# A shift of 224 bytes for the split weights that TensorE holds

## The chip, the cores and the metric

The kernel runs on one core of one Trainium2 chip. The core has a matrix engine (TensorE, PE in the profile; its weight loads are shown apart as PEld), a vector engine (VectorE, DVE), an activation engine (ScalarE, ACT), GpSimd (POOL) and a queue engine (SyncE, SP) that issues most DMAs. The on-chip memory SBUF has 128 partitions; a "byte offset" below always means an offset within each partition. The metric is the device time of one execution in microseconds (us); smaller is better.

## What is computed

Two transformer layers run over 256 tokens of width 2048, batch 1. Cut to what matters:

```python
# layer 1
hn = rms_norm(h, norm_mix);  h = h + nsa_mixer(hn, ...)            # compressed/selected/window attention
hn = rms_norm(h, norm_ffn);  h = h + square(relu(hn @ ffn_w1)) @ ffn_w2     # 2048 -> 8192 -> 2048
gate = sigmoid(rms_norm(h, norm_ple) @ ple_w_gate);  h = h + (p @ ple_w_proj) * gate
x = rms_norm(h, norm_final)
# layer 2
x = x + rms_norm(swa_sink_attention(rms_norm(x, g0), ...), g1)     # window 128, 32 heads
x = x + rms_norm(conv_ffn(rms_norm(x, g2), w_up, conv, w_down), g3)  # 2048 -> 2*5632 -> 2048
```

All is float32, and the products have to be nearly of float32 precision. Nearly all the work is products of the 256 token columns with about 400 MB of weights, each weight used once.

## The kernel before

The weights lie in DRAM as one stream of 128 x 128 tiles in the order of their use (`_stream`). `Weights.load` brings 16 tiles (1 MB) at a time into `w_raw`. `Weights.split` takes units of 8 tiles and writes each as two float32r numbers into one of four `w_split` buffers: the rounded value `hi` (ScalarE, L243) and the rest `lo` (VectorE, L244). A buffer holds 8 tiles of `hi` (4096 bytes) and behind them 8 tiles of `lo` (4096 bytes). The activations are split likewise: a `slot`, `h` or `o` tile holds 256 columns of `hi` and 256 of `lo`. A product is then hi·hi + hi·lo + lo·hi.

TensorE multiplies a stationary operand (128 columns, brought into the array by a LDWEIGHTS) with a moving one (up to 512 columns that stream past it). Three helpers use the weights:

- `mm` (L296 to L303): the weight tile is stationary and the activations move. Each tile costs one **pair**: `hi` held against 512 columns (L302), then `lo` held against 256 (L303). The result comes out transposed, as the next layer's input needs it. 3152 pairs.
- `mm_beside` (L305 to L313): the same with four output banks side by side, at the start of both feed-forward parts. 128 pairs.
- `mm_rows` (L315 to L325; `mm_rows_last` L327 to L337): the activations are stationary, and 4 weight tiles (512 columns) move, three matmuls for each half of the tokens. In `compress` (L809) the weights move too.

While a matmul streams, the LDWEIGHTS of the next one runs beside it. Tiles' places are set by pools in order of allocation. `pad` tiles (L457, L504, L560, L606, L610, L1098) fill up to multiples of 256 bytes (`ALIGN`): in the built program `w_split`, `slot`, `h`, `o`, `q`, `kh` and `vh` all begin at a multiple of 256 bytes, so that the stationary and the moving operand of every `mm`, `mm_beside` and `mm_rows` matmul stand at the same offset modulo 256, namely 0. Constants such as the identity stand at 224.

`hz` (L858, L1120) is the hidden activation before its split into `h`; it lies in the pool `base`, two buffers, through `tmp`.

The order on each engine is the order of the code, with a few places moved by `issue_after`.

Of the kernel before, what the change touches and what calls it, by code (L numbers as in the profile page):

```python
# [13 lines left out]
P = 128  # L14
S = 256
# [29 lines left out]


ALIGN = 256


V_MIX, V_FFN, V_PLE, V_FIN = 0, 16, 32, 48  # L50
# [44 lines left out]
    return [(i, NFF2 + i) for i in range(q * QUART, (q + 1) * QUART)]  # L95


def _stream(a):

    w = a["nsa_w_in"][0]  # L100
    kv = {n: w[:, 2048 + 512 * i : 2560 + 512 * i] for i, n in enumerate(("kc", "vc", "ks", "vs", "kw", "vw"))}
    out = [_g_major(kv["vs"]), _g_major(kv["vw"])]
    gates = np.zeros((KD, P, P), np.float32)
    gates[:, :, :48] = w[:, 5120:5168].reshape(KD, P, 48)
    out.append(gates)
    tiles = [_m_major(kv[n]).reshape(G, KD, P, P) for n in ("kc", "vc", "ks", "kw")]
    q = _m_major(w[:, :2048]).reshape(4 * G, KD, P, P)
    w1k, w1v = (a[f"nsa_cmp_w1_{n}"][0].reshape(4, CMP_L // 4, P, P) for n in "kv")
    out += list(tiles[0])
    for c in range(4):  # L110
        out += [tiles[1][c], w1k[c]]
    for c, t in enumerate((tiles[2][0], tiles[3][0], q[0], q[1])):
        out += [t, w1v[c]]
    out += list(q[2:4])
    for g in range(1, G):
        out += [tiles[2][g], tiles[3][g], *q[4 * g : 4 * g + 4]]
    out.append(_g_major(a["nsa_w_out"][0]))
    for h in range(2):
        w = a["ffn_w1"][0][:, h * 4096 : (h + 1) * 4096]
        if h == 0:  # L120
            out.append(_g_major(w[:, :COLS]))
            w = w[:, COLS:]
        out.append(_m_major(w))
        out.append(_g_major(a["ffn_w2"][0][h * 4096 : (h + 1) * 4096]))
    gate = _g_major(a["ple_w_gate"][0]).reshape(NG, -1, P, P)
    proj = _g_major(a["ple_w_proj"][0]).reshape(NG, -1, P, P)
    out.append(np.concatenate([gate, proj], axis=1).reshape(-1, P, P))
    w = a["swa_w_in_2"][0]
    order = _swa_order()
    out.append(_g_major(w[:, 2560:3072]))  # L130
    out.append(_m_major(w[:, 2048:2560]))
    out.append(_m_major(w[:, :2048][:, order]))
    out.append(_g_major(a["swa_w_out_2"][0][order]))
    up = a["ffn_w_up_2"][0].reshape(KD, P, 2 * NFF2, P)
    down = a["ffn_w_down_2"][0]

    def ups(pairs):
        return up[:, :, [m for pair in pairs for m in pair]]

    first = _conv_tiles(0)  # L140
    out.append(ups(first[:2]).transpose(0, 2, 1, 3).reshape(-1, P, P))
    out.append(ups(first[2:]).transpose(2, 0, 1, 3).reshape(-1, P, P))
    for q in range(4):
        nxt = _conv_tiles(q + 1) if q < 3 else []
        if nxt:
            out.append(ups(nxt[:1]).transpose(2, 0, 1, 3).reshape(-1, P, P))
        out.append(_g_major(down[q * QUART * P : (q + 1) * QUART * P]))
        if nxt:
            out.append(ups(nxt[1:]).transpose(2, 0, 1, 3).reshape(-1, P, P))
    n = sum(len(b) for b in out)  # L150
    pad = -n % 16
    flat = np.concatenate(out + [np.zeros((pad, P, P), np.float32)])
    return np.ascontiguousarray(flat.reshape(-1, 16, P, P).transpose(0, 2, 1, 3)).reshape(-1, P, 16 * P), n


def _cols(v):
# [50 lines left out]
class Weights:  # L207


    def __init__(self, nc, pool, src, blocks):  # L210
        self.nc, self.pool, self.src = nc, pool, src
        self.n, self.units = src.shape[0], -(-blocks // UNIT)
        self.at = self.n_dma = self.n_split = 0
        self.raw, self.both = {}, {}
# [18 lines left out]
    def split(self, upto):  # L233
        nc = self.nc
        while self.n_split < min(upto, self.units):
            u = self.n_split
            self.load(u // 2 + 1)
            raw = self.raw[u // 2][:, (u % 2) * UNIT * P : (u % 2 + 1) * UNIT * P]
            both = self.pool.tile([P, 2, UNIT * P], F32R, tag="w_split", name=f"w_split{u}", bufs=W_SPLIT)
            hi, lo = both[:, 0], both[:, 1]  # L240
            half = UNIT * P // 2
            for c in (slice(0, half), slice(half, 2 * half)) if u == 0 else (slice(0, 2 * half),):
                nc.scalar.activation(hi[:, c], raw[:, c], AF.Copy)  # L243
                nc.vector.tensor_tensor(lo[:, c], raw[:, c], hi[:, c].bitcast(F32), op=ALU.subtract)  # L244
            self.both[u] = both
            self.n_split += 1
            if u % 2:
                self.raw.pop(u // 2)
                self.load(u // 2 + 1 + W_RAW)
# [14 lines left out]


class Program:
    def __init__(self, tc, ins, out, blocks):
        self.tc, self.nc, self.ins, self.out, self.blocks = tc, tc.nc, ins, out, blocks
        self.uid = 0


# [180 lines left out]
    def build(self):  # L452
        tc, nc, ins = self.tc, self.nc, self.ins
        self.base = tc.alloc_tile_pool(name="base", bufs=1)
        self.psum = tc.alloc_tile_pool(name="psum", bufs=1, space=bass.MemoryType.PSUM)
        self.dram = tc.alloc_tile_pool(name="dram", bufs=1, space=bass.MemoryType.DRAM)
        self.pad(self.base, 64)  # L457
        self.w = Weights(nc, self.base, ins["w"], self.blocks)

        self.vecs = self.tile(self.base, [P, NV], F32, "vecs")  # L460
        cst = self.tile(self.base, [P, NC_], F32, "cst")
        self.ident = cst[:, C_ID : C_ID + P]
        self.ones = cst[:, C_ONE : C_ONE + P]
        self.fold = cst[:, C_FOLD : C_FOLD + 64]
        self.mask = cst[:, C_MASK : C_MASK + S]
        self.cmask = cst[:, C_CMASK : C_CMASK + 32].rearrange("p (b n) -> p b n", b=2)
        self.cvalid = cst[:, C_CVALID : C_CVALID + 32].rearrange("p (b n) -> p b n", b=2)

        self.eps = self.tile(self.base, [P, 1], F32, "eps")
        nc.vector.memset(self.eps, EPS)  # L470
        nc.scalar.dma_start(self.vecs[:, :KD], ins["vec"][:, :KD])
        self.x_pool = x_pool = tc.alloc_tile_pool(name="x0", bufs=1, side="right")
        x0 = [self.tile(x_pool, [P, 2, S], F32, f"x{i}") for i in range(KD // 2)]

        def load_x(i):
            nc.sync.dma_start(x0[i], ins["x"][:, 2 * i : 2 * i + 2])

        self.w.load(W_RAW, load_x)
        for i in range(2 * W_RAW, KD // 2):
            load_x(i)  # L480
        nc.scalar.dma_start(cst, ins["cst"])
        nc.scalar.dma_start(self.vecs[:, KD:], ins["vec"][:, KD:])


        idle = self.tile(x_pool, [P, COLS], F32R, "idle")
        nc.vector.memset(idle.bitcast(F32), 0.0)
        ps = self.ps_mm()
        for i in range(WARM):
            nc.tensor.matmul(ps, lhsT=idle[:, :P], rhs=idle, start=True, stop=True)


        xs = []
        acc = self.tile(x_pool, [P, S], F32, "acc")
        self.ps_vs = [self.ps_att(), self.ps_att()]
        for k in range(KD):
            src = x0[k // 2][:, k % 2]
            if k % 2 == 0:
                self.w.split(k // 2 + 1)
            x = self.slot(k, F32R)
            self.split512(x, src, self.vec(V_MIX + k))  # L500
            self.add_square(acc, src, k == 0)
            xs.append(x)
            self.mm_rows(self.ps_vs, [x], k == 0, k == KD - 1)
        self.pad(self.base, 96)  # L504
        self.nsa(xs, acc)
        self.ffn()
        self.ple()
        self.swa()
        self.conv_ffn()
        for pool in (self.pool_z, self.pool_y, self.dram, self.psum, self.base):  # L510
            pool.release()
        assert self.w.at == self.blocks
# [325 lines left out]
    def ffn(self):  # L838
# [8 lines left out]
        for part in range(2):  # L847
            hs = []
            beside = self.mm_beside(xs) if part == 0 else []
            for m in range(half):  # L850
                if m < len(beside):
                    ps = beside[m]
                else:
                    ps = self.ps_mm()
                    self.mm(ps, xs)
                z = self.total(ps)
                h = self.tmp("hz", 2)
                nc.vector.scalar_tensor_tensor(h, z, 0.0, z, op0=ALU.max, op1=ALU.mult)  # L858
                hr = self.tile(pool, [P, 512], F32R, f"h{m}")
                self.split512(hr, h)  # L860
                hs.append(hr)
# [229 lines left out]
    def conv_ffn(self):  # L1091
# [23 lines left out]
        def hidden(i, ps_g, ps_v):  # L1115
            cg, cv = conv(ps_g, i), conv(ps_v, NFF2 + i)
            sg = self.tile(pool, [P, S], F32, "sg", 2)
            nc.scalar.activation(sg, cg, AF.Silu)
            h = self.tmp("hz", 2)
            nc.vector.tensor_tensor(h, sg, cv, op=ALU.mult)  # L1120
            hs[i] = self.tile(pool, [P, 512], F32R, "h", QUART + 3)
            self.split512(hs[i], h)
# [97 lines left out]
```

## Time and profile before

| what | value |
|---|---|
| time, median of 3 runs | 2269.18 us (2268.64 to 2269.22) |
| time of the profiled execution | 2269.81 us |
| its span, first to last instruction | 2268.0 us |
| mean granted TensorE clock | 0.997 of full speed |
| matmuls of `mm` (L302, L303) | 3152 and 3152 |
| matmuls of `mm_rows` (L323 to L325) | 4032 |
| busy, PE / DVE / ACT / POOL | 99% / 64% / 52% / 11% |

PE is the engine that is busy all the time; DVE and ACT follow with the split of the weights. A matmul's duration in the profile holds its way through the array, so consecutive ones overlap: the pace of a stream is the distance from start to start, not the duration.

### The profile page before, as it was taken

The page shows a single profiled execution, that of the slowest core. Times are in us where ns is not written, and L with a number is a line of the kernel's source. Part 1 is how long each engine was busy: PE and PEld are TensorE (multiplying, and loading weights), DVE is VectorE, ACT ScalarE, POOL GpSimd, SP SyncE. Part 2 cuts the span into 40 slices and gives each one's busy share as a digit, 9 for nine tenths or more (in the row PEclk, how much of TensorE's full clock was granted, in tenths as well). Part 3 has the DMA queues.
Part 4 walks back from the last instruction along what each step waited for, and adds up shares of the span by engine and source line. Part 5 has one row for each costly group of instructions (what it writes and reads, how often), then busy time and mean ns, then how long its engine had stood idle before and what let it go on. Part 6 is the DMA issues. An engine that isn't in the chain of part 4 may idle for free. (4 is left out here: it accounts for less than half of the span.)

```text
span 2268.0 us, 29986 instructions
## 1 busy us (share of the span) xinstructions
PE 2236.1 (99%) x11645; PEld 1892.5 (83%) x11645; DVE 1447.1 (64%) x2181; ACT 1181.1 (52%) x1894; POOL 243.2 (11%) x309
## 2 busy tenths in 40 slices
PE   8999999999999999999999999999999999999998
PEld 6888887888888888888888888778888888888886
DVE  7676665566544566644566777567756766765775
ACT  4566554444433444444465566456545544554554
POOL 5432210000000000000001123002100100110110
PEclk9999999999999999999999999999999999999999
DMA  6553335555555555555555544445555555555553
GB/s 254 196 199 127 123 128 213 185 201 186 196 192 191 197 186 187 186 186 188 212 191 185 204 142 165 167 147 189 187 195 189 188 186 186 186 189 200 186 186 130
DMA packets 65950, 415.64 MB, mean 183 GB/s; under 512 B 7408, under 2 KB 12528, under 8 KB 17424
## 3 DMA queue, kind: packets, MB, share of 16 engines
q1 hardware_dynamic: 65376, 413.01, 50.5%
q8 instruction: 91, 1.49, 0.2%
q10 hardware_dynamic: 432, 0.73, 0.1%
q14 instruction: 51, 0.42, 0.0%
HBM read 410.03 MB, written 3.67 MB: 182 GB/s over the span
## 5 line engine op out<-in xcount | busy, mean ns | idle before, releaser
L244 DVE TENSOR_TENSOR w_split<-w_raw,w_split 128x1024 fp32r<-128x1024 f32 (+1 forms) x759 | 946.4, 1248 | 641.9 <-ACT w_split L243 636.4
L243 ACT ACTIVATE w_split<-w_raw 128x1024 fp32r<-128x1024 f32 (+1 forms) x759 | 801.6, 1057 | 699.4 <-PE att L325 447.9
L302 PE MATMUL mm<-slot,w_split 128*128 128x512 f32 x3152 | 1117.3, 399 | 1.5 <-DVE z L346 1.5
L303 PE MATMUL mm<-slot,w_split 128*128 128x256 f32 x3152 | 885.2, 281 | 0.0
L302 PEld LDWEIGHTS mm<-slot,w_split 128*128 128x128 f32 x3152 | 592.0, 188 | 149.8 <-issue 3.4
L303 PEld LDWEIGHTS mm<-slot,w_split 128*128 128x128 f32 x3152 | 595.3, 189 | 0.3
L324 PE MATMUL att<-w_split,h 128*128 128x512 f32 x848 | 330.2, 389 | 0.0
L325 PE MATMUL att<-w_split,h 128*128 128x512 f32 x848 | 330.2, 389 | 0.0
L323 PE MATMUL att<-w_split,h 128*128 128x512 f32 x848 | 330.1, 389 | 0.0
L344 ACT ACTIVATE t<-mm 128x256 f32<-128x256 f32 x201 | 76.4, 381 | 228.5 <-PE mm L303 227.0
L325 PEld LDWEIGHTS att<-w_split,h 128*128 128x128 f32 x848 | 159.2, 188 | 33.1
L324 PEld LDWEIGHTS att<-w_split,h 128*128 128x128 f32 x848 | 159.2, 188 | 32.9
L323 PEld LDWEIGHTS att<-w_split,h 128*128 128x128 f32 x848 | 159.2, 188 | 32.8
L1107 POOL TENSOR_TENSOR u<-z,rb 128x256 f32<-128x256 f32 x88 | 71.0, 808 | 694.3 <-DVE z L346 585.3
L346 DVE TENSOR_TENSOR z<-mm,t 128x256 f32<-128x256 f32 x201 | 84.8, 423 | 79.8 <-ACT t L344 79.8
L324 PE MATMUL att<-w_split,slot 128*128 128x512 f32 x320 | 125.9, 393 | 4.0 <-DVE w_split L244 3.9
L323 PE MATMUL att<-w_split,slot 128*128 128x512 f32 x320 | 125.2, 393 | 1.8 <-ACT w_split L243 1.7
L325 PE MATMUL att<-w_split,slot 128*128 128x512 f32 x320 | 125.7, 393 | 0.0
L919 POOL MEMSET vh<- 128x512 f32 x1 | 0.5, 524 | 910.1 <-DVE sum L391 910.1
L324 PEld LDWEIGHTS att<-w_split,slot 128*128 128x128 f32 x320 | 60.4, 189 | 19.2 <-DVE w_split L244 6.8
L323 PEld LDWEIGHTS att<-w_split,slot 128*128 128x128 f32 x320 | 60.3, 189 | 15.1 <-ACT w_split L243 3.0
L325 PEld LDWEIGHTS att<-w_split,slot 128*128 128x128 f32 x320 | 60.4, 189 | 12.2
(261 smaller groups left out, 1901.0 us busy)
## 6 DMA issues: line engine op xcount, KB each, us to landing
w_raw<-in_w SPq DMA_DIRECT2D x376, 1024.0 KB, 4.8
bias<-bandd SPq DMA_DIRECT2D x32, 128.0 KB, 2.7
w_raw<-in_w SPq DMA_DIRECT2D x5, 512.0 KB, 7.6
x<-in_x SPq DMA_DIRECT2D x8, 256.0 KB, 6.9
slot<-in_xn SPq DMA_DIRECT2D x8, 256.0 KB, 7.9
gain<-in_rows SPq DMA_DIRECT2D x2, 1024.0 KB, 6.1
out<-slot SPq DMA_DIRECT2D x8, 256.0 KB, 2.0
bandd<-rows SPq DMA_DIRECT2D x2, 768.0 KB, 6.4
```

The lines of the kernel that those rows point to most:

```text
L243: nc.scalar.activation(hi[:, c], raw[:, c], AF.Copy)
L244: nc.vector.tensor_tensor(lo[:, c], raw[:, c], hi[:, c].bitcast(F32), op=ALU.subtract)
L302: nc.tensor.matmul(ps, lhsT=hi, rhs=x, start=i == 0, stop=False)
L303: nc.tensor.matmul(ps[:, S:], lhsT=lo, rhs=x[:, :S], start=False, stop=i == n - 1)
L323: nc.tensor.matmul(ps[b], lhsT=xh, rhs=hi, start=first and i == 0, stop=False)
L324: nc.tensor.matmul(ps[b], lhsT=xh, rhs=lo, start=False, stop=False)
L325: nc.tensor.matmul(ps[b], lhsT=xl, rhs=hi, start=False, stop=last and i == n - 1)
L344: nc.scalar.activation(t, ps[:, S : 2 * S], AF.Copy)
L346: nc.vector.tensor_tensor(z, ps[:, :S], t, op=ALU.add)
L919: nc.gpsimd.memset(t[:, :, :, 64:128].bitcast(F32), 0.0)
L1107: nc.gpsimd.tensor_tensor(u[:, 2:], self.total(ps), rb, op=ALU.mult)
```

## The change

Each unit of 8 tiles gets a mark, `held`: 1 if its weights will be stationary (used by `mm` or `mm_beside`), 0 if they will move (`mm_rows`, `compress`). `_stream` returns the marks beside the data; the data and their order are the same. A `w_split` buffer grows by 256 bytes, from 8192 to 8448, and a unit with mark 1 is written, and then read, 56 floats (224 bytes) further on in it. Units with mark 0 stay at the buffer's start. To make room, `hz` moves from the pool `base` into the pools of the two feed-forward stages, again with two buffers.

In the built program the order of the instructions on each of the five engines is the same as before, row for row. The operands of matmuls keep their offsets modulo 256, save the held weights, which go from 0 to 224, both `hi` and `lo`. `hz` goes from 96 to 0. One wait is placed otherwise: the first `hz` of the first feed-forward waits for POOL as well as for DVE, and the first `h` behind it waits no longer for POOL.

```diff
+SHIFT = 56
 def _stream(a):
-    out = [_g_major(kv["vs"]), _g_major(kv["vw"])]
+    out.add(0, _g_major(kv["vs"]), _g_major(kv["vw"]))
-    out.append(gates)
+    out.add(1, gates)
...
-        out.append(_m_major(w))
-        out.append(_g_major(a["ffn_w2"][0][h * 4096 : (h + 1) * 4096]))
+        out.add(1, _m_major(w))
+        out.add(0, _g_major(a["ffn_w2"][0][h * 4096 : (h + 1) * 4096]))
...
+class _Parts(list):
+    def add(self, held, *parts):
+        for b in parts:
+            assert len(b) % UNIT == 0
+            self.append(b)
+            self.held.extend([held] * (len(b) // UNIT))
 class Weights:
     def split(self, upto):
-            both = self.pool.tile([P, 2, UNIT * P], F32R, tag="w_split", name=f"w_split{u}", bufs=W_SPLIT)
+            both = self.pool.tile([P, 2 * UNIT * P + ALIGN // 4], F32R, tag="w_split", name=f"w_split{u}",
+                                  bufs=W_SPLIT)
+            at = SHIFT * self.held[u]
+            both = both[:, at : at + 2 * UNIT * P].rearrange("p (a n) -> p a n", a=2)
             hi, lo = both[:, 0], both[:, 1]
 # ffn (L858) and conv_ffn (L1120)
-                h = self.tmp("hz", 2)
+                h = self.tile(pool, [P, S], F32, "hz", 2)
```

## Rows read from the trace of the kernel before

**Rows 1.** The page: span, busy time of PE, slices of POOL (40 equal ones)

```profile
span 2268.0 us, 29986 instructions
...
PE 2236.1 (99%) x11645; PEld 1892.5 (83%) x11645; DVE 1447.1 (64%) x2181; ACT 1181.1 (52%) x1894; POOL 243.2 (11%) x309
...
POOL 5432210000000000000001123002100100110110
```

**Rows 2.** The page's costliest groups: count, busy us, mean ns, idle before

```profile
L244 DVE TENSOR_TENSOR w_split<-w_raw,w_split 128x1024 fp32r<-128x1024 f32 (+1 forms) x759 | 946.4, 1248 | 641.9 <-ACT w_split L243 636.4
L243 ACT ACTIVATE w_split<-w_raw 128x1024 fp32r<-128x1024 f32 (+1 forms) x759 | 801.6, 1057 | 699.4 <-PE att L325 447.9
L302 PE MATMUL mm<-slot,w_split 128*128 128x512 f32 x3152 | 1117.3, 399 | 1.5 <-DVE z L346 1.5
L303 PE MATMUL mm<-slot,w_split 128*128 128x256 f32 x3152 | 885.2, 281 | 0.0
L302 PEld LDWEIGHTS mm<-slot,w_split 128*128 128x128 f32 x3152 | 592.0, 188 | 149.8 <-issue 3.4
```

**Rows 3.** Groups by shape, the pairs of mm_beside, engine PE

```profile
L312 PE MATMUL mm<-slot,w_split 128*128 128x512 f32 x64 | 25.3, 421 | 0.0
L312 PE MATMUL att<-slot,w_split 128*128 128x512 f32 x64 | 23.8, 400 | 0.0
```

**Rows 4.** Windows: engines' busy us (instructions), PEclk, DMA share, GB/s

```profile
460.00:560.00 100.00, 100.00 (x567) 86.74 (x567) 64.34 (x90) 49.62 (x72) 0.00 (x0) 1.00 0.54 195
630.00:730.00 100.00, 100.00 (x443) 82.80 (x442) 49.33 (x43) 38.62 (x38) 0.00 (x0) 1.00 0.53 189
```

**Rows 5.** Timeline, engine PE, first feed-forward: start us, us, line, tiles, shape

```profile
835.66 0.40 PE L302 MATMUL mm<-slot,w_split 128*128 128x512 f32 x1
...
836.02 0.40 PE L302 MATMUL mm<-slot,w_split 128*128 128x512 f32 x1
...
836.37 0.40 PE L302 MATMUL mm<-slot,w_split 128*128 128x512 f32 x1
...
836.72 0.40 PE L302 MATMUL mm<-slot,w_split 128*128 128x512 f32 x1
...
841.67 0.40 PE L302 MATMUL mm<-slot,w_split 128*128 128x512 f32 x1
```

**Rows 6.** Timeline, engine PE, the keys of the second layer, 13 pairs

```profile
1259.74 0.39 PE L302 MATMUL mm<-slot,w_split 128*128 128x512 f32 x1
...
1264.25 0.39 PE L302 MATMUL mm<-slot,w_split 128*128 128x512 f32 x1
```

**Rows 7.** Timeline, engine PE, a stretch of mm_rows, 11 matmuls

```profile
699.82 0.39 PE L324 MATMUL att<-w_split,h 128*128 128x512 f32 x1
...
702.31 0.39 PE L323 MATMUL att<-w_split,h 128*128 128x512 f32 x1
```

**Rows 8.** Start of conv_ffn: the window (columns as above), timeline of PE

```profile
1516.60:1518.40 1.80, 1.80 (x8) 1.57 (x7) 1.80 (x6) 1.07 (x3) 0.00 (x0) 0.50 0.05 9
...
1517.27 0.63 PE L312 MATMUL mm<-slot,w_split 128*128 128x512 f32 x1
1517.70 0.41 PE L313 MATMUL mm<-slot,w_split 128*128 128x256 f32 x1
1517.91 0.63 PE L312 MATMUL mm<-slot,w_split 128*128 128x512 f32 x1
```

**Rows 9.** Timeline, engine PE, two places where constants or sums are loaded next

```profile
58.44 0.40 PE L325 MATMUL att<-w_split,slot 128*128 128x512 f32 x1
58.68 0.28 PE L376 MATMUL att<-cst,acc 128*128 128x2 f32 x2
...
1541.90 0.29 PE L313 MATMUL att<-slot,w_split 128*128 128x256 f32 x1
1542.02 0.59 PE L446 MATMUL att<-diag,cst 128*128 128x256 f32 x2
```

More of the change, by code (lines that the diff above doesn't have):

```diff
@@ L95, in _conv_tiles, with __init__ @@
     return [(i, NFF2 + i) for i in range(q * QUART, (q + 1) * QUART)]
+class _Parts(list):
+    def __init__(self, held):
+        self.held = held
+    def add(self, held, *parts):
[3 more added lines that the diff above has]
+            self.held.extend([held] * (len(b) // UNIT))
 def _stream(a):
+    held = []
+    out = _Parts(held)
     w = a["nsa_w_in"][0]
     kv = {n: w[:, 2048 + 512 * i : 2560 + 512 * i] for i, n in enumerate(("kc", "vc", "ks", "vs", "kw", "vw"))}
-    out = [_g_major(kv["vs"]), _g_major(kv["vw"])]
+    out.add(0, _g_major(kv["vs"]), _g_major(kv["vw"]))
     gates = np.zeros((KD, P, P), np.float32)
     gates[:, :, :48] = w[:, 5120:5168].reshape(KD, P, 48)
-    out.append(gates)
+    out.add(1, gates)
     tiles = [_m_major(kv[n]).reshape(G, KD, P, P) for n in ("kc", "vc", "ks", "kw")]
@@ L108, in _stream @@
     w1k, w1v = (a[f"nsa_cmp_w1_{n}"][0].reshape(4, CMP_L // 4, P, P) for n in "kv")
-    out += list(tiles[0])
+    out.add(1, *tiles[0])
     for c in range(4):
-        out += [tiles[1][c], w1k[c]]
+        out.add(1, tiles[1][c])
+        out.add(0, w1k[c])
     for c, t in enumerate((tiles[2][0], tiles[3][0], q[0], q[1])):
-        out += [t, w1v[c]]
-    out += list(q[2:4])
+        out.add(1, t)
+        out.add(0, w1v[c])
+    out.add(1, *q[2:4])
     for g in range(1, G):
-        out += [tiles[2][g], tiles[3][g], *q[4 * g : 4 * g + 4]]
-    out.append(_g_major(a["nsa_w_out"][0]))
+        out.add(1, tiles[2][g], tiles[3][g], *q[4 * g : 4 * g + 4])
+    out.add(0, _g_major(a["nsa_w_out"][0]))
     for h in range(2):
@@ L120, in _stream @@
         if h == 0:
-            out.append(_g_major(w[:, :COLS]))
+            out.add(1, _g_major(w[:, :COLS]))
             w = w[:, COLS:]
-        out.append(_m_major(w))
-        out.append(_g_major(a["ffn_w2"][0][h * 4096 : (h + 1) * 4096]))
+        out.add(1, _m_major(w))
+        out.add(0, _g_major(a["ffn_w2"][0][h * 4096 : (h + 1) * 4096]))
     gate = _g_major(a["ple_w_gate"][0]).reshape(NG, -1, P, P)
     proj = _g_major(a["ple_w_proj"][0]).reshape(NG, -1, P, P)
-    out.append(np.concatenate([gate, proj], axis=1).reshape(-1, P, P))
+    out.add(0, np.concatenate([gate, proj], axis=1).reshape(-1, P, P))
     w = a["swa_w_in_2"][0]
     order = _swa_order()
[L130 to L133, printed above, removed]
+    out.add(0, _g_major(w[:, 2560:3072]))
+    out.add(1, _m_major(w[:, 2048:2560]))
+    out.add(1, _m_major(w[:, :2048][:, order]))
+    out.add(0, _g_major(a["swa_w_out_2"][0][order]))
     up = a["ffn_w_up_2"][0].reshape(KD, P, 2 * NFF2, P)
@@ L140, in _stream @@
     first = _conv_tiles(0)
-    out.append(ups(first[:2]).transpose(0, 2, 1, 3).reshape(-1, P, P))
-    out.append(ups(first[2:]).transpose(2, 0, 1, 3).reshape(-1, P, P))
+    out.add(1, ups(first[:2]).transpose(0, 2, 1, 3).reshape(-1, P, P))
+    out.add(1, ups(first[2:]).transpose(2, 0, 1, 3).reshape(-1, P, P))
     for q in range(4):
@@ L145, in _stream @@
         if nxt:
-            out.append(ups(nxt[:1]).transpose(2, 0, 1, 3).reshape(-1, P, P))
-        out.append(_g_major(down[q * QUART * P : (q + 1) * QUART * P]))
+            out.add(1, ups(nxt[:1]).transpose(2, 0, 1, 3).reshape(-1, P, P))
+        out.add(0, _g_major(down[q * QUART * P : (q + 1) * QUART * P]))
         if nxt:
-            out.append(ups(nxt[1:]).transpose(2, 0, 1, 3).reshape(-1, P, P))
+            out.add(1, ups(nxt[1:]).transpose(2, 0, 1, 3).reshape(-1, P, P))
     n = sum(len(b) for b in out)
@@ L152, in _stream @@
     flat = np.concatenate(out + [np.zeros((pad, P, P), np.float32)])
-    return np.ascontiguousarray(flat.reshape(-1, 16, P, P).transpose(0, 2, 1, 3)).reshape(-1, P, 16 * P), n
+    return np.ascontiguousarray(flat.reshape(-1, 16, P, P).transpose(0, 2, 1, 3)).reshape(-1, P, 16 * P), n, held
 def _cols(v):
@@ L207, with __init__ @@
 class Weights:
-    def __init__(self, nc, pool, src, blocks):
-        self.nc, self.pool, self.src = nc, pool, src
+    def __init__(self, nc, pool, src, blocks, held):
+        self.nc, self.pool, self.src, self.held = nc, pool, src, held
         self.n, self.units = src.shape[0], -(-blocks // UNIT)
@@ L266, with __init__ @@
 class Program:
-    def __init__(self, tc, ins, out, blocks):
-        self.tc, self.nc, self.ins, self.out, self.blocks = tc, tc.nc, ins, out, blocks
+    def __init__(self, tc, ins, out, blocks, held):
+        self.tc, self.nc, self.ins, self.out, self.blocks, self.held = tc, tc.nc, ins, out, blocks, held
         self.uid = 0
@@ L457, in build @@
         self.pad(self.base, 64)
-        self.w = Weights(nc, self.base, ins["w"], self.blocks)
+        self.w = Weights(nc, self.base, ins["w"], self.blocks, self.held)
         self.vecs = self.tile(self.base, [P, NV], F32, "vecs")
@@ L1118, in hidden @@
             nc.scalar.activation(sg, cg, AF.Silu)
-            h = self.tmp("hz", 2)
+            h = self.tile(pool, [P, S], F32, "hz", 2)
             nc.vector.tensor_tensor(h, sg, cv, op=ALU.mult)
@@ L1195 @@
     cst, band = _constants()
-    w, blocks = _stream(a)
+    w, blocks, held = _stream(a)
     arrays = {
@@ L1215 @@
         if True:
-            Program(tc, ins, out, blocks).build()
+            Program(tc, ins, out, blocks, held).build()
     r = run_bass_kernel_spmd(nc, [{f"in_{k}": v for k, v in arrays.items()}], core_ids=[0])
```

## The prediction

> **What bounds the kernel now.** I read the page first: PE is busy for 2236.1 of 2268.0 us [rows 1]. So only a faster PE makes the kernel faster, and only if its matmuls come at a quicker pace. The costliest groups say where PE's time lies: 3152 pairs in `mm` (L302, L303), whose idle time before them is 1.5 us in all [rows 2]. With 64 + 64 pairs in `mm_beside` [rows 3] that is 3280 pairs in which a weight tile is stationary. These are the matmuls that the change touches; it leaves `mm_rows` as it is.
>
> Durations are of no use for the pace, since neighbours overlap (399 + 281 = 680 ns for a pair, and yet 100 us hold 567 matmuls [rows 2, 4]). So I went to the timeline and took start to start. In the first feed-forward the first and the last row are 17 pairs apart: 6.01 us / 17 = **353.5 ns** a pair [rows 5]. The reader is to see the rhythm there: steps of 0.36, 0.35, 0.35 us that repeat.
>
> What would a pair take without any stall? At the start of `conv_ffn`, behind transposes that waited, PE ran for some us at granted clock 0.50, that is 1.2 GHz. There a pair takes 0.43 + 0.21 = 0.64 us [rows 8], which is 768 columns at one column a cycle, with the same loads beside it and nothing lost. At 2.4 GHz the same count gives 320 ns. So 33.5 ns a pair, 110 us over 3280 pairs, are lost at the full clock only. `mm_rows` loses less: 2.49 us / 11 = 226.4 ns a matmul [rows 7] against 213.3, so 13.1 ns for each weight load, where a pair of `mm` has 16.8.
>
> The loss isn't fixed by the instructions. For the keys of the second layer the same code, with all operands at the same offsets modulo 256, goes at 4.51 us / 13 = **346.9 ns** a pair [rows 6]. Two loads at 13.1 ns make 320 + 26.2 = 346.2, so this is the pace at which a load in `mm` costs what it costs in `mm_rows`. So there are two rhythms into which the stream can fall, and which one depends on how the reads of the held weights (LDWEIGHTS, 188 ns [rows 2]) lie in time against the reads of the moving operand. That is what a shift of one of the two addresses could change: it acts like a delay of one stream of reads against the other.
>
> The Trainium skill, "TensorE: Matmul & The Clock Gate", section "Back-to-back issue gap", gives N / 2.4 + 2.5 ns for a matmul at the full clock; estimated by it a pair would take 325 ns, so it has 28 of the 33.5 ns unexplained, and the trace doesn't agree with it for float32r.
>
> **The change part by part.**
>
> *Held weights at 224 instead of 0.* No instruction comes or goes, and none changes its place. What may change is the stall of the 3280 pairs. The trace before has no steady stream with the held operand at another offset than the moving one, so I bound it by rows:
> - from below, no stall: 320 ns, -33.5 ns a pair, -110 us.
> - from above, the longest step in the slow rhythm, 0.36 us [rows 5], for every pair: about +7 ns, +23 us. The only loads at 224 beside a moving operand at 0 that the trace has say the same: a 512 column matmul with such a load behind it takes 58.44 to 58.68, 0.24 us, and a 256 column one 1541.90 to 1542.02, 0.12 us [rows 9], together 0.36. They are single, and the load is of another kind (a plain float32 operand), so they count for little.
> - between them the quick rhythm, 346.9 ns, which the same code reaches now and then. I take this one: it is the one pace besides the present that `mm` is seen to hold, and `mm_rows` holds its equal all the time. Looking along the timeline I put a tenth of the pairs in it already (a choice; most long stages show the slow one). 0.9 x 3280 x 6.6 ns = 19.5 us.
>
> *The split writes to the new place* (L243, L244, 759 each; 1057 and 1248 ns [rows 2]). Cost 0: in a stretch of `mm` DVE is busy for 64 and ACT for 50 of 100 us [rows 4], so both stay ahead of PE even if a write took a third longer; without that cover, 100 ns more on L244 would be at most 76 us. The first units move and aren't shifted, so the start, where PE does wait for the splits, stays as it is.
>
> *A quicker PE asks for more data.* 2% more of the 195 GB/s in `mm` is 199, at a DMA share of 0.54, and DVE goes from 64 to 66 of 100 us [rows 4]. Nothing is late next.
>
> *`hz` in other pools.* It has two buffers as before, and its instructions stay. The first `hz` of the feed-forward waits for POOL instead of the `h` behind it; POOL is idle in fifteen slices from the seventh on (from 340 us, a slice being 56.7) [rows 1], and the feed-forward begins inside them. 0 us; if it did wait, once, about 1 us.
>
> **The sum.** The profiled execution took 2269.81 us (span 2268.0, and 1.8 around it), 0.6 above the median of the runs, 0.03%. 2269.81 - 19.5 = 2250.3 for a profiled execution, and 2269.18 - 19.5 = 2249.7, so **2250 us** for the median.
>
> **The rivals.**
>
> *The loads get clear of the moving reads altogether.* Then the pair goes towards 320 ns. For it: the half clock shows that nothing but this rate of reading stands in the way. Against it: `mm_rows`, too, keeps 13.1 ns a load for hundreds of us and never gets below. With half of the stall gone (336.8 ns) it is -55 us, 2214; with all of it 2159. Chance 0.17.
>
> *Nothing happens.* If what a load costs is a slot taken from the moving stream whatever the addresses, the shift does nothing, and the rhythm stays what the sequence of lengths 512, 256 makes it: 2269. For it: pairs at the same offsets take two paces, so something besides the address picks the pace. Against it: the two paces show that the mutual position of the reads counts. Chance 0.13. The Trainium skill speaks for this rival: "SBUF — State Buffer", section "Who interferes with whom", gives TensorE two read ports, one for the moving operand and one for LDWEIGHTS, independent of each other. By that rule the offset of one against the other cannot matter. The trace agrees at the half clock and not at the full one, where 33.5 ns a pair are lost.
>
> *Slower: the load behind the short matmul comes late.* The load lasts 188 ns, the step of a 256 column matmul beside which it runs only some 0.12 us [rows 9]. So that load has no cover to give away: a load that meets more of the moving reads at 224 ends later, and the next 512 column matmul starts later by as much. The place is the step L303 to L302; the price is that of the pair at 0.36 us, +7 ns, 2292; half of it is 2281. It decides from a pair of 354.9 ns on (+1.4 ns, +4.5 us). For it: the two steps behind a load at 224 [rows 9], and that equal offsets hold everywhere now, so that any other relation is untried in this trace. Against it: the slow rhythm already has the steps of 0.36 us, so most of that price is paid. Chance 0.24.
>
> **How the numbers follow.** Forecast 0.46 (a gain of 5 to 35 us, 2234 to 2264), clear 0.17, nothing 0.13, slower 0.24. What a measurement of this kernel can tell from no change is about 0.2%, 4.5 us. Faster: 0.46 + 0.17 = 0.63; same: 0.13; slower: 0.24. For the range I go down past the middle of the clear case to 2190, which leaves out the lower part of it (0.08), and up to 2286, which leaves out the upper part of the slower case (0.09). The forecast's own range is 2234 to 2264.
>
> **What the profile afterwards would show.** Right: in the timeline of the first feed-forward, 17 pairs take 5.9 us instead of 6.01, in even steps of 0.35 us; 100 us of `mm` hold about 577 matmuls; the LDWEIGHTS of L302 and L303 stay at 188 ns; `mm_rows` stays at 226.4 ns; DVE's and ACT's split durations don't move. Clear: pairs below 340 ns. Slower: steps of 0.36 us or more in every pair, most of it between L303 and the next L302. Nothing: 0.36, 0.35, 0.35 again. Wrong in another way: `mm_rows` changes its pace though its operands keep their offsets, or PE shows idle time behind L243 or L244 in the `mm` stages.

## The result and the profile after

The changed kernel takes 2253.72 us (median of 6 runs, 2251.93 to 2255.68), the kernel before, run beside it, 2269.2. The ratio is 0.9928, with a 95% interval of 0.9915 to 0.9941: 0.7% faster, 13 to 19 us. The forecast was 2250.0.

The code lies 22 lines further down: L324 and L325 are the pair of `mm`, L345 to L347 `mm_rows`, L265 and L266 the split. The page of the kernel after, its span, its busy engines and the groups that answer to [rows 1, 2]:

```profile
span 2251.0 us, 29986 instructions
...
PE 2219.1 (99%) x11645; PEld 1897.0 (84%) x11645; DVE 1444.9 (64%) x2181; ACT 1180.1 (52%) x1894; POOL 244.7 (11%) x309
...
L266 DVE TENSOR_TENSOR w_split<-w_raw,w_split 128x1024 fp32r<-128x1024 f32 (+1 forms) x759 | 946.5, 1248 | 628.6 <-ACT w_split L265 622.8
L265 ACT ACTIVATE w_split<-w_raw 128x1024 fp32r<-128x1024 f32 (+1 forms) x759 | 801.2, 1057 | 685.0 <-PE att L347 446.1
L324 PE MATMUL mm<-slot,w_split 128*128 128x512 f32 x3152 | 1100.5, 392 | 1.5 <-DVE z L368 1.5
L325 PE MATMUL mm<-slot,w_split 128*128 128x256 f32 x3152 | 889.8, 282 | 0.0
L324 PEld LDWEIGHTS mm<-slot,w_split 128*128 128x128 f32 x3152 | 592.5, 188 | 128.9 <-issue 3.4
```

The span is 17.0 us shorter and PE's busy time 17.0. The rest kept its size: the split takes 1248 and 1057 ns as before, the load 188 ns, the idle time before L324 is 1.5 us. What is left is the time from one matmul's start to the next one's. The timeline of PE after, in the first feed-forward at the place of [rows 5] (start us, duration us, then line and tiles), and below it a stretch of `mm_rows`, the place of [rows 7]:

```profile
835.28 0.39 PE L324 MATMUL mm<-slot,w_split 128*128 128x512 f32 x1
...
835.63 0.39 PE L324 MATMUL mm<-slot,w_split 128*128 128x512 f32 x1
...
835.97 0.39 PE L324 MATMUL mm<-slot,w_split 128*128 128x512 f32 x1
...
841.17 0.39 PE L324 MATMUL mm<-slot,w_split 128*128 128x512 f32 x1
```

```profile
699.19 0.39 PE L346 MATMUL att<-w_split,h 128*128 128x512 f32 x1
...
701.91 0.39 PE L346 MATMUL att<-w_split,h 128*128 128x512 f32 x1
```

The first and the last row of the first fence are 17 pairs apart: 5.89 us / 17 = **346.5 ns** where it was 353.5. The steps are even; the one of 0.36 us that came every third time is gone. `mm_rows` has 12 matmuls in 2.72 us, 226.7 ns: unchanged. The windows of the kernel after say the same in counts, where [rows 4] had 567 and 443 (us, then busy us and instructions of PE, PEld, DVE, ACT, POOL, then PEclk, DMA share, GB/s); the third window is a place where the clock fell:

```profile
460.00:560.00 100.00, 100.00 (x579) 88.67 (x578) 65.40 (x92) 50.52 (x73) 0.00 (x0) 1.00 0.56 198
630.00:730.00 100.00, 100.00 (x442) 82.79 (x442) 48.66 (x44) 39.26 (x37) 0.00 (x0) 1.00 0.54 196
...
268.00:271.30 3.30, 3.30 (x15) 2.91 (x15) 3.23 (x20) 2.47 (x12) 0.00 (x0) 0.56 0.29 119
```

Taken over the whole trace, from the start of each matmul to the start of the next: L302's steps sum to 748.8 us before and L324's to 727.1 after; L303's 370.7 became 375.7; `mm_rows` went from 931.6 to 931.0. So the pairs of `mm` give back 16.7 of the 17.0 us. The long matmul's step got shorter by 6.9 ns, the short one's longer by 1.6.

### The profile page after: what moved, and what is told of

It is laid out like the page before. It is cut to its first block, busy times and chain, and to the rows that moved or that the text cites. A ratio compares the mean times of both kernels' runs of the same rounds, so it can differ in the third digit from the quotient of the medians.

```text
span 2251.0 us, 29986 instructions
## 1 busy us (share of the span) xinstructions
PE 2219.1 (99%) x11645; PEld 1897.0 (84%) x11645; DVE 1444.9 (64%) x2181; ACT 1180.1 (52%) x1894; POOL 244.7 (11%) x309
## 5 line engine op out<-in xcount | busy, mean ns | idle before, releaser
L266 DVE TENSOR_TENSOR w_split<-w_raw,w_split 128x1024 fp32r<-128x1024 f32 (+1 forms) x759 | 946.5, 1248 | 628.6 <-ACT w_split L265 622.8
L265 ACT ACTIVATE w_split<-w_raw 128x1024 fp32r<-128x1024 f32 (+1 forms) x759 | 801.2, 1057 | 685.0 <-PE att L347 446.1
L324 PE MATMUL mm<-slot,w_split 128*128 128x512 f32 x3152 | 1100.5, 392 | 1.5 <-DVE z L368 1.5
L325 PE MATMUL mm<-slot,w_split 128*128 128x256 f32 x3152 | 889.8, 282 | 0.0
L324 PEld LDWEIGHTS mm<-slot,w_split 128*128 128x128 f32 x3152 | 592.5, 188 | 128.9 <-issue 3.4
L325 PEld LDWEIGHTS mm<-slot,w_split 128*128 128x128 f32 x3152 | 596.4, 189 | 0.3
L347 PE MATMUL att<-w_split,h 128*128 128x512 f32 x848 | 330.2, 389 | 0.0
L345 PE MATMUL att<-w_split,h 128*128 128x512 f32 x848 | 330.0, 389 | 0.0
L345 PEld LDWEIGHTS att<-w_split,h 128*128 128x128 f32 x848 | 159.2, 188 | 33.2
L347 PEld LDWEIGHTS att<-w_split,h 128*128 128x128 f32 x848 | 159.2, 188 | 32.8
L345 PE MATMUL att<-w_split,slot 128*128 128x512 f32 x320 | 125.2, 393 | 1.8 <-ACT w_split L265 1.8
L347 PE MATMUL att<-w_split,slot 128*128 128x512 f32 x320 | 125.9, 393 | 0.0
L345 PEld LDWEIGHTS att<-w_split,slot 128*128 128x128 f32 x320 | 60.4, 189 | 15.3 <-ACT w_split L265 2.9
L347 PEld LDWEIGHTS att<-w_split,slot 128*128 128x128 f32 x320 | 60.3, 189 | 12.2
```

Source lines behind the costliest of these rows:

```text
L324: nc.tensor.matmul(ps, lhsT=hi, rhs=x, start=i == 0, stop=False)
L325: nc.tensor.matmul(ps[:, S:], lhsT=lo, rhs=x[:, :S], start=False, stop=i == n - 1)
L345: nc.tensor.matmul(ps[b], lhsT=xh, rhs=hi, start=first and i == 0, stop=False)
L347: nc.tensor.matmul(ps[b], lhsT=xl, rhs=hi, start=False, stop=last and i == n - 1)
```

## The experiments

The theory under test (A): the place of the held operand against that of the moving one, modulo 256 bytes, sets how long a load stops the stream of matmuls. The rivals came one by one; each is named where it is tested. Paces are start to start.

**1. The shift alone set to 0, all else as changed.** It parts A from the rival that the wider buffer or `hz`'s new place did it.

```diff
-SHIFT = 56
+SHIFT = 0
```

> The changed kernel with a shift of 0 bytes: larger buffers and hz's new place stay, the held weights go back to offset 0. Theory A (the offset of the held operand against the moving one, modulo 256, sets the rhythm of the pairs): the time of before, 2269 us (2266 to 2272), pairs at 353.5 ns in steps of 0.36, 0.35, 0.35 us. Rival B (the buffers' new pitch of 8448 bytes, or hz's place, made the gain): stays at 2254 us (2251 to 2257), pairs at 347 ns. A mix of both: in between, and the share of each is read off.

Measured: 2271.61 us, ratio to before 1.0 (0.9992 to 1.0009). The timeline at the same place:

```profile
835.11 0.40 PE L324 MATMUL mm<-slot,w_split 128*128 128x512 f32 x1
...
841.12 0.40 PE L324 MATMUL mm<-slot,w_split 128*128 128x512 f32 x1
```

17 pairs in 6.01 us, 353.5 ns. The whole gain is the shift; that rival falls.

**2. A ladder of shifts for the held weights within one run**, `h` half by half and stage by stage: `ladder` gives the units of a stretch the shifts of its list one after the other.

```diff
+LADDER2 = (0, 8, 16, 24, 32, 40, 48, 56)   # in floats; others likewise
...
-        out.add(1, _m_major(w))
+        out.ladder((LADDER1, LADDER2)[h], _m_major(w))
```

> The changed kernel, but in both halves of the first feed-forward and in conv_ffn the held weights stand at a row of shifts, from 0 to 256 bytes, 32 to 64 pairs each; the pace of each stretch is read from the trace. Theory A with banks of 32 bytes or more: the pace is a function of the shift, 353 ns at 0 and at 256, 347 ns at 224, other values elsewhere, some slower than 353; a shift has the same pace wherever it comes in the program. Rival C (any shift away from equal offsets breaks the slow rhythm): 347 ns at every shift but 0 and 256. Rival D (what matters is how a stretch is entered, since before showed both paces at shift 0): the same shift gives 347 in one stretch and 353 in another. Time of the whole between 2250 and 2275 us.

Measured (pair of L335, L336): 353.1 to 353.6 ns at 32, 64, 80, 112, 192 and 240; 346.6 or 346.7 at 8, 16, 48, 96 and 224; 349 to 351 at 4, 128, 144, 160, 176, 208, 216 and 232. At 0 it was 353.3 in all its places, but 346.7 at 256, which is the same offset modulo 256. The timeline at 64 bytes (17 pairs from the first row) and at 96 (17 again):

```profile
819.69 0.40 PE L335 MATMUL mm<-slot,w_split 128*128 128x512 f32 x1
...
825.70 0.40 PE L335 MATMUL mm<-slot,w_split 128*128 128x512 f32 x1
...
844.67 0.39 PE L335 MATMUL mm<-slot,w_split 128*128 128x512 f32 x1
...
850.56 0.39 PE L335 MATMUL mm<-slot,w_split 128*128 128x512 f32 x1
```

6.01 against 5.89 us: no order by size, and 224 is one of several good places. Rival C falls, since 32, 64, 112, 192 and 240 gain nothing; rival D is not ruled out for equal offsets, since 0 and 256 differ.

**3. The same ladder for the moving weights of `mm_rows`.**

```diff
-        out.add(0, _g_major(a["ffn_w2"][0][h * 4096 : (h + 1) * 4096]))
+        out.ladder((LADDER1, LADDER2)[h], _g_major(a["ffn_w2"][0][h * 4096 : (h + 1) * 4096]))
```

> The changed kernel, but the moving weights of the first feed-forward's second product and of conv_ffn's down products stand at a row of shifts from 0 to 256 bytes; held weights stay at 224. Theory A: mm_rows' 226.5 ns a matmul depends on the shift too, with some shifts slower (up to 236 ns, the slowest steps seen) and perhaps one quicker; the held operand is at 0 there, so a moving shift of 32 bytes is the same relation as a held shift of 224. Rival D2 (a stream of equal matmuls always falls into the same rhythm): 226.5 ns at every shift. Time between 2250 and 2275 us.

Measured, ns a matmul: 226.7 at 0 and 112, 228.8 at 64, 231 to 232 at 16 and 80, 233 to 234 at 8, 32, 48, 96, 128, 160, 176, 192 and 224, 236.7 at 4 and 240. The timeline at 0 (9 matmuls from the first to the second row) and at 32 (9 from the third to the fourth):

```profile
599.79 0.39 PE L356 MATMUL att<-w_split,h 128*128 128x512 f32 x1
...
601.83 0.39 PE L356 MATMUL att<-w_split,h 128*128 128x512 f32 x1
...
625.30 0.40 PE L356 MATMUL att<-w_split,h 128*128 128x512 f32 x1
...
627.40 0.39 PE L356 MATMUL att<-w_split,h 128*128 128x512 f32 x1
```

2.04 against 2.10 us. Rival D2 falls: `mm_rows` depends on the offset, too, and at 0 it already has the best one: a shift for the moving weights, too, would have cost time.

**4. The kernel before, with the pool `base` begun 32 bytes later.** Held and moving operands that both lie in it keep their relation at another absolute place; those with one partner in it change it. The second pad is 32 bytes shorter, so that what lies behind it stays.

```diff
-        self.pad(self.base, 64)
+        self.pad(self.base, 96)
...
-        self.pad(self.base, 96)
+        self.pad(self.base, 64)
```

> The kernel before, with the base pool (w_split, and slots 0 to 15) moved by 32 bytes and all that lies behind it left in place. In the first layer and in conv_ffn both operands of mm stand at 32, so their relation is still 0; in the second layer's attention (slots 24 to 39) the held weights stand at 32 and the moving operand at 0; in mm_rows over h the weights move at 32 and the held operand stands at 0. Theory A (relation): 353 ns a pair in both feed-forwards as before. Rival E (the absolute place of the held weights): another pace there, the same as in the second layer's attention. mm_rows over h shows what a relation of 224 does to it.

Measured: 2288.53 us. The timeline of `mm` in the first feed-forward, both operands at 32 (17 pairs), and of `mm_rows` with the moving operand at 32 and the held one at 0 (9 matmuls):

```profile
835.38 0.40 PE L302 MATMUL mm<-slot,w_split 128*128 128x512 f32 x1
...
841.39 0.40 PE L302 MATMUL mm<-slot,w_split 128*128 128x512 f32 x1
...
699.52 0.40 PE L325 MATMUL att<-w_split,h 128*128 128x512 f32 x1
...
701.62 0.39 PE L325 MATMUL att<-w_split,h 128*128 128x512 f32 x1
```

6.01 us / 17 = 353.5 ns, as at 0 and 0; 2.10 us / 9 = 233.3 ns, as at relation 32 or 224 in the run before. With both at 32, `mm_rows` over the slots had 226.8, as at 0 and 0. It is `mm_rows` that parts A from rival E: with the moving weights at 32 both times, the pace goes with the held operand's place. `mm` alone would not part them, since by experiment 2 a relation of 32 has 353 as well. The relation counts, not the absolute place. (In the first stage of `conv_ffn` 320 pairs with both at 32 went at 346.7, so this relation has both paces here, too.)

**5. Streams by themselves**, 48 matmuls each at the kernel's start: widths (512), (512, 256) or (256), held columns 128, 64 or 32, shift 0 or 224. It asks whether the loss is a number of columns read by the load (F) or a fixed one (G).

```diff
+        for widths, held, at in PROBES:
+            for i in range(48):
+                n = widths[i % len(widths)]
+                nc.tensor.matmul(ps[:held, :n], lhsT=probe[:, at : at + held], rhs=probe[:, :n], start=True, stop=True)
```

> The changed kernel with thirteen streams of 48 matmuls on zeros put in behind the warm-up; their results go to a bank that nobody reads. Moving widths 512, 256 or both in turn; 128, 64 or 32 held columns; held offset 0 or 224 bytes against the moving one. Theory F (in the quick rhythm a load takes reading time from the moving stream in proportion to what it reads): 512 columns take 226.5 ns with 128 held columns, 220 with 64, 216.5 with 32; pairs of 512 and 256 take 347 ns with 128 held columns at 224, and about 333 with 64. Rival G (a fixed price for each change of the held operand): 226.5 ns and 347 ns whatever the number of held columns. Both: pairs with 128 held columns at 0 in steps of 0.36, 0.35, 0.35 us, 353 ns, or 347 if the entry decides. For 512 alone at 224 held the shift of 32 in the moving operand had 233 ns: the same here. The whole takes 100 to 130 us more than the changed kernel.

The timeline rows hold whole runs of equal matmuls (start us, us from the first's start to the last's end, shape, count). In order: 128 held columns at 0, 32 at 0, 128 at 224; then pairs with 128 at 0 and with 64 at 0:

```profile
10.65 5.83 PE L525 MATMUL mm<-probe 128*128 128x512 f32 x25
...
32.67 6.18 PE L525 MATMUL mm<-probe 128*32 128x512 f32 x26
...
43.83 6.23 PE L525 MATMUL mm<-probe 128*128 128x512 f32 x26
...
75.83 4.63 PE L525 MATMUL mm<-probe 128*128 128x512 f32 x25
...
91.83 5.49 PE L525 MATMUL mm<-probe 128*64 128x512 f32 x31
```

Without the last one's 0.39 us (0.39 for the pairs too, which end on a long matmul): 5.44 / 24 = 226.7 ns, 5.79 / 25 = 231.6, 5.84 / 25 = 233.6; pairs 4.24 / 12 = 353.3 and 5.10 / 15 = 340.0. The pair at 224 took 346.7, with 128 held columns and with 64. A load of 32 columns lasts 108 ns, one of 128 columns 188, yet it is the shorter that costs more here, while in the pairs at 0 the 64 columns cost less. F falls: it had 216.5 ns for 32 columns and 333 for the pairs with 64 at 224. G in its plain form falls too: the offset changes the cost with all lengths the same. The first two streams and a part of the third still had work of the kernel beside them; the window of the pairs with 128 columns at 0 has none (us, busy us and instructions of PE, PEld, DVE, ACT, POOL, then PEclk, DMA share, GB/s):

```profile
72.00:80.70 8.70, 8.70 (x51) 7.45 (x49) 0.00 (x0) 0.00 (x0) 0.00 (x0) 1.00 0.01 2
```

The window of the pairs at 224 has none either. So 353.3 and 346.7 belong to TensorE's own stream.

**6. How a stretch is entered.** Relation 0 and 256 behind other shifts. Theories: both rhythms keep themselves and the entry picks one, the quick one behind 96 (A2); 256 differs from 0 (H); it always falls back to the slow one (I).

```diff
+LADDER5 = (2, 0, 12, 0, 24, 0, 64, 0)   # in floats; others likewise
-            out.add(1, ups(nxt[1:]).transpose(2, 0, 1, 3).reshape(-1, P, P))
+            out.ladder((LADDER4, LADDER5, LADDER6)[q], ups(nxt[1:]).transpose(2, 0, 1, 3).reshape(-1, P, P))
```

> The changed kernel with other rows of shifts: stretches at 0 (or 256) bytes that follow a stretch at 96, 224, 16, 8 or 48 bytes in the same run of mm. Theory A2 (at offset 0 the stream has two rhythms that both hold themselves, and the phase at entry decides): the stretch at 0 behind one at 96 bytes runs at 347 ns to its end, even over 400 pairs; behind 224 at 353 ns. Rival H (256 isn't the same as 0, which is why the one stretch at 256 was quick): 256 quick behind any shift, 0 slow behind any. Rival I (offset 0 always falls back into the slow rhythm after some pairs): 353 ns at the end of each long stretch. 8 and 32 bytes of the table: 16, 32 and 128 floats aren't in it; 32 bytes behind 96 and behind 224 may differ (352 and 347 have both been seen).

The timeline at shift 0 behind 96, twice: in the second feed-forward half (17 pairs), and in the convolution's (16 pairs from the third row to the fourth):

```profile
814.69 0.40 PE L334 MATMUL mm<-slot,w_split 128*128 128x512 f32 x1
...
820.70 0.40 PE L334 MATMUL mm<-slot,w_split 128*128 128x512 f32 x1
...
1965.83 0.39 PE L334 MATMUL mm<-slot,w_split 128*128 128x512 f32 x1
...
1971.38 0.39 PE L334 MATMUL mm<-slot,w_split 128*128 128x512 f32 x1
```

6.01 / 17 = 353.5 ns and 5.55 / 16 = 346.9, with the same offsets. The slow stretch lasts 440 pairs in one place, the quick one 120 (at 0, 256 and 0 again), until the relation changes. 256 was quick behind 96 and slow behind 96, too. So the first half of A2 holds, that either rhythm keeps itself; H and I fall. The second half missed: behind 96 the 440 pairs were expected at 347 ns and ran at 353.3, so the shift before doesn't decide alone. That the entry picks the rhythm is argued from this; nothing here shows what does.

**7 and 8. Every held weight at 96, and every held weight at 64.** By experiment 2 one is good and one is not. The rivals: 224 is special (J); any shift but 0 helps (C).

```diff
-SHIFT = 56
+SHIFT = 24
```
```diff
-SHIFT = 56
+SHIFT = 16
```

> The changed kernel with all held weights at 96 bytes instead of 224. Theory A with the table of paces: 346.6 ns a pair in every stage, so the time of the changed kernel, 2254 us (2251 to 2257). Rival J (224 is special, as 32 bytes short of the next buffer line): pairs above 350 ns in some stages and 2262 us or more.

> The changed kernel with all held weights at 64 bytes. Theory A with the table: 353.1 ns a pair, so no gain against the kernel before: 2270 us (2266 to 2273), though the relation isn't 0. Rival C (any shift away from equal offsets helps): 2254 us.

Measured: 96 bytes 2252.96 us, ratio 0.9921 (0.9908 to 0.9933); 64 bytes 2273.39, ratio 1.0009 (1.0 to 1.0018). The timelines at the same place as ever, 17 pairs each, first with 96:

```profile
835.37 0.39 PE L324 MATMUL mm<-slot,w_split 128*128 128x512 f32 x1
...
841.26 0.39 PE L324 MATMUL mm<-slot,w_split 128*128 128x512 f32 x1
```

and with 64:

```profile
835.36 0.40 PE L324 MATMUL mm<-slot,w_split 128*128 128x512 f32 x1
...
841.37 0.40 PE L324 MATMUL mm<-slot,w_split 128*128 128x512 f32 x1
```

5.89 and 6.01 us. J and C fall: the same code, the same buffers, and 20 us between two shifts.

**9. A map**, every shift in steps of 4 bytes, held ones in `mm` and moving ones in `mm_rows`.

```diff
+MAP1 = tuple(range(0, 14))     # up to MAP5 and 63
+ROWS1 = tuple(range(0, 32))    # ROWS2: 32 to 63
...
```

> The changed kernel with a finer table: held weights at every multiple of 4 bytes from 0 to 252 in the feed-forwards (24 to 32 pairs each), and moving weights at every multiple of 4 bytes in the first feed-forward's second products (24 matmuls each). Theory K (each matmul at full clock has a least loss of 13.3 ns with 128 held columns, and the shift only adds to it): no pair below 346.5 ns, no matmul of mm_rows below 226.5 ns at any shift. Rival L (some shift, not tried yet, frees the loads): a pair below 345 ns somewhere.

Measured: no pair below 346.4 ns; 346.6 at 16 of the 64 places (0 among them this time, behind 224), most others 348 to 353, the worst about 364 at 60 and 360 at 156. `mm_rows`: none below 226.5; 226.7 at 0, up to 240.0 at 20, 100, 228 and 244. Some places read otherwise than before (8, 176, 232 and 240 in experiment 2; 112 for `mm_rows`, 231.1 here and 226.7 in experiment 3), so more offsets than 0 have two paces. It left open whether 346.6 is the least there is (K).

**10 and 11. `hi` and `lo` at different shifts**, 58 choices, then 80 more, and with these (96, 240) again at ten places.

```diff
...
-            hi, lo = both[:, 0], both[:, 1]
+            hi, lo = both[:, at : at + n], both[:, n + low : 2 * n + low]
...
```

> The changed kernel with hi and lo of the held weights at different shifts in the feed-forwards: hi at 0, 32, 64, 96, 128, 160 or 224 bytes and lo at a row of multiples of 16 or 8 bytes from there up. hi is loaded beside the 256 column matmul and lo beside the 512 column one. Theory K: no pair below 346.5 ns, and quick and slow pairs mixed. Rival L: a choice of the two that frees both loads, 340 ns or less, which would be worth some 22 us more if it held everywhere.

> The changed kernel with 80 further choices of the shifts of hi and lo (multiples of 16 bytes, lo at or behind hi), 24 to 32 pairs each, and hi at 96, lo at 240 bytes, which had 343.3 ns in the table before, put in ten times between others. If 343.3 ns is a rhythm of that choice: at most of the ten places. If it depends on the entry: at some of them, 346.6 or more at the others. Theory K was wrong about 346.6 being the least; with a least loss of another kind some choice may go to 340 ns, which would be 22 us.

Measured: nearly all choices between 346.5 and 353.6. (96, 240) gave 343.3 ns, then 343.2 to 343.5 at nine places of ten and 351.5 at the tenth; (176, 208) gave 343.3 at its one place. Nothing was quicker. The timeline of the second of the two runs at one of the nine places (12 pairs), then at the tenth (17):

```profile
477.76 0.39 PE L345 MATMUL mm<-slot,w_split 128*128 128x512 f32 x1
...
481.88 0.39 PE L345 MATMUL mm<-slot,w_split 128*128 128x512 f32 x1
...
881.66 0.40 PE L345 MATMUL mm<-slot,w_split 128*128 128x512 f32 x1
...
887.63 0.39 PE L345 MATMUL mm<-slot,w_split 128*128 128x512 f32 x1
```

4.12 / 12 = 343.3 and 5.97 / 17 = 351.2 ns. K falls, and this choice has two rhythms as well.

**12. All held weights at (96, 240).**

```diff
+APART = (24, 60)
...
-            self.held.extend([held] * (len(b) // UNIT))
+            self.held.extend([APART if held else 0] * (len(b) // UNIT))
...
```

> All split weights that are held: the high part 96 bytes into its buffer, the low part 240 bytes into its own, the pair that took 343.2 to 343.5 ns at nine of its ten places of the run before, and 351.5 ns at the tenth. Theory A (the place of the held operand against the moving one, modulo 256 bytes, sets each of the two steps of a pair, and a rhythm once taken is kept): 343.3 ns instead of 346.9 in all 3280 pairs, 3.6 ns x 3280 = 11.8 us under the changed kernel, 2242 us. If the rhythm in which a stretch is entered decides, as at the tenth place, a tenth to a half of the pairs lie at 351.5: 2244 to 2256 us. Theory K (346.6 ns is the least that a pair can take, and 343.3 ns was a matter of short stretches): 2253 us.

Measured: 2250.48 us (2248.08 to 2252.68), ratio to before 0.9915 (0.99 to 0.993). The timeline in the first feed-forward's first half (17 pairs), then in its second (17):

```profile
499.85 0.40 PE L338 MATMUL mm<-slot,w_split 128*128 128x512 f32 x1
...
505.82 0.39 PE L338 MATMUL mm<-slot,w_split 128*128 128x512 f32 x1
...
835.39 0.39 PE L338 MATMUL mm<-slot,w_split 128*128 128x512 f32 x1
...
841.23 0.39 PE L338 MATMUL mm<-slot,w_split 128*128 128x512 f32 x1
```

351.2 ns in the one, 343.5 in the other. The first half stays at the slow rhythm for its 448 pairs of `mm`, the second at the quick one for its 512; over the trace 2337 of the 3152 pairs lie in stages at 343.3 and 788 in stages at 351. That is the case in which the entry decides (2244 to 2256), not the 2242 of a rhythm that is always the quick one. Its profiled execution is 4.7 us below the changed kernel's (1.5 of it a place of low clock that the latter had alone, see below), but the intervals of the two ratios overlap, so the kernel isn't shown to be faster than the change.

## Why the prediction was right

*What bounds the kernel.* Right. The pace of the pairs moved, PE stayed at 99%, and the time followed: 16.7 of 17.0 us.

*The quick rhythm as the value taken.* Right in the pace, in part by luck: 346.5 ns forecast as 346.9, 579 matmuls in 100 us forecast as about 577, steps of 0.35 us. The mechanism stands in this form: at offsets 0 and 0 the stream has two rhythms that keep themselves [rows 5, 6], and experiments 2 and 6 showed either at the same offsets; at 224 only the quick one showed, in every stage of ten pairs or more of the kernel after (346.7 ns, one 347.2 behind the low clock) and wherever experiments 2, 6 and 9 used 224. It is not that the loads got clear, and not that 0 is bad: 64 is as bad, and 0 can be as good. But nothing in the prediction said why 224 should be an offset that has the quick rhythm: it took the one other pace that it had seen. In the map 16 of 64 offsets ran at it, so that part was luck. That the shift acts as a delay of one stream of reads against the other isn't shown either.

*The sum.* 19.5 us forecast, 15.5 by the medians, 17.1 by the profiled executions. "A tenth of the pairs in it already" was a good choice: counted by stages, 2808 pairs of `mm` ran in the slow rhythm before and 310 in the quick one. The slow stages gave back 18.2 us, 6.5 ns a pair, and the pairs of `mm_beside` 0.8: 19.0 together. What the sum didn't have is a fall of the clock. At 268 us of the kernel after, behind 3 us in which PE had been busy for 1.34 (it waited 1.66 us for ACT's `pth`, L728), the granted clock was 0.56 over the window shown, near the lower level (1.2 GHz); five pairs took 0.64 to 0.78 us, and the stage took 1.5 us longer than before. The rest of the steps lost 0.4 us, which leaves 17.1. The fall is not shown to come of the change. The kernel before waits at the same place for 1.67 us, and its clock stayed up:

```profile
270.20:273.50 3.30, 3.30 (x23) 2.95 (x23) 3.26 (x20) 2.38 (x11) 0.00 (x0) 1.00 0.29 122
```

Experiment 8, all in the slow rhythm, shows the fall at this place (0.56 over 271.0 to 274.3 us), and experiment 12 does not (1.00 over 268.0 to 271.3).

*The bounds.* The lower one, 320 ns, was never reached: the least in any run is 340.0, with 64 held columns, and 343.3 in the kernel. The upper one, "the longest step in the slow rhythm, 0.36 us", was no bound: shift 60 has about 364 ns a pair, its longest step being 0.39. The singles behind a load at 224 [rows 9] said 0.36 us for the pair and were rightly given little weight.

*The split, the data and `hz` at no cost.* Right: 1248 and 1057 ns, DVE at 65 and ACT at 51 of 100 us in `mm`, 198 GB/s; experiment 1 bears these edits alone at a ratio of 1.0.

*The rival in which nothing happens.* Wrong: the pace goes with the offset. The time that it gave exists, at the shift of 64 bytes, but not for its reason. The Trainium skill, "SBUF — State Buffer", section "Who interferes with whom", has the two read ports of TensorE independent. By that rule 64 and 96 bytes would take one time; the runs differ by 20 us, so for float32r matmuls in this kernel the measurement decides against it.

*The pair of 325 ns.* The Trainium skill's formula behind it is given in "TensorE: Matmul & The Clock Gate", section "Back-to-back issue gap", for a single matmul by itself. The prediction set it against a stream, which here took 346.6 to 353.5; nothing in the sum hangs on it.

*The slower rival.* Its place was real and its price small: the step from the short matmul to the next long one did grow, by 1.6 ns (375.7 against 370.7 us over 3152), under the 6.9 ns that the other step gave back.

*What stays open.* Why a load stops the stream at all (13.3 ns in `mm_rows` at its best, 11.7 a load in the pairs at 343.3), and what in the chip the offset acts upon; the runs show the law by paces alone. What picks the rhythm on entering a stretch is not found either; the shift before it doesn't do so alone.

## What to carry to other kernels

In a stream of float32r matmuls that keeps PE busy, measure the pace from start to start and compare it with the columns over the clock; where it is above, try a few offsets of one operand against the other in different stretches of one run, since the order is not to be guessed (96 good, 64 bad). Then run the best at full length: a short stretch shows a rhythm that can be held, not the one that the kernel will enter. And look at each kind of matmul apart: here the shift that helps `mm` would have cost `mm_rows` 6.7 ns a matmul.

## What was not expected of the hardware

- The same instructions at the same offsets have two steady rhythms, 346.6 and 353.3 ns a pair, and keep either for a hundred pairs and more (440 and 120 in experiment 6, 0 and 256 taken as one offset).
- The cost of a load is no measure of its length: beside 512 moving columns a load of 32 columns (108 ns) makes 231.6 ns, one of 128 columns (188 ns) 226.7, at equal offsets; in pairs at equal offsets 64 held columns make 340.0 ns and 128 make 353.3.
- The offset of a single operand moves a 512-column matmul between 226.7 and 240.0 ns, and a pair between 346.6 and about 364 (343.3 with `hi` and `lo` at different shifts), in steps as small as 4 bytes.
- At the lower clock (1.2 GHz) nothing of the loss is left: 0.64 us a pair, 768 columns at one a cycle, at 268 us in the kernel after, with the held weights at 224, as in [rows 8] with 0.
